# Second mixer's norm: TensorE sums each block's squares itself, with 10 waking instructions in place of 28

## Chip, cores and metric

The kernel runs on one core of a Trainium2 chip. The metric is the device time of one execution in microseconds (us). Before the change the median of three runs is 1398.13 us (1397.18 to 1398.22).

## What is computed

Two decoder layers on 512 tokens of 1024 features. Each layer is a mixer and a mixture of experts (MoE), each behind an RMS norm and with a residual; a last RMS norm follows. Layer 0's mixer is a gated MLP beside a short convolution, layer 1's is a gated linear recurrence. Cut to the part that matters here:

```python
def rms_norm(x, g):
    xf = x.astype(jnp.float32)
    y = xf * lax.rsqrt(jnp.mean(jnp.square(xf), axis=-1, keepdims=True) + EPS)
    return y.astype(x.dtype) * g

for layer in range(DEPTH):
    h = rms_norm(x, norm_mix_g[layer])
    if layer % 2 == 0:
        x = x + mixer_ab(h, ...)          # layer 0
    else:
        x = x + mixer_rglru(h, ...)       # layer 1: the "second mixer"
    h = rms_norm(x, norm_ffn_g[layer])
    x = x + hierarchical_moe(h, ...)      # 32 experts, 2 per token
return rms_norm(x, norm_final_g)
```

The change is at the RMS norm ahead of `mixer_rglru`: for every token the 1024 squares of x have to be summed.

## The kernel before

Between the stages x stands transposed, in `xT`: 8 blocks of 128 features (partitions) by 512 tokens. The stages follow each other: mixer 0 (0 to 129 us), its output projection with the routing of tokens to experts (to 198 us), MoE 0 (to 690 us), mixer 1, its projection and routing (to 896 us), MoE 1 and the last norm (to 1399 us). All weights arrive through one stream of 1 MB loads on SyncE's queue, which runs ahead through a ring of ten buffers: a load starts when the work before it has freed a slot.

**Around the change.** The last experts of MoE 0 are added to x in eight steps (`combine`, L992 and L993). Step i makes the 128x512 product `pc` of block i on TensorE (two matmuls of 512 columns, in fp32r), VectorE adds it to `xT`, and then `after(i)` runs, which here is an object of the class `Sums`. It has ScalarE square block i into `sq[i]` (four buffers, `i % 4`). The four blocks 0 to 3 are added on GpSimd into one (three additions of 128x512), the blocks 4 to 7 on VectorE into another (three more). TensorE then sums each of the two over the 128 partitions: `square_sums` (L327) makes four matmuls, one for 128 tokens each, in which the squares are the stationary 128x128 operand and the column `one` is the moving one. Every fp32 matmul of the program stands in the trace as two MATMUL and two LDWEIGHTS, so one call of `square_sums` is eight of each.

`wake(b, n)` (L170) issues n matmuls of the 128x128 identity whose result nobody reads. After the first `square_sums` stand nine (18 instructions in the trace), after the second five (10). The table `WAKE` holds these counts.

Then `rstd_of` (L308) turns the sums into 1/sqrt(mean + eps): VectorE scales the sums and adds eps (L311), ScalarE takes the root (L317), VectorE inverts it and refines it by a Newton step (L318 to L321). `Normed` spreads the result with four transposes on TensorE (`prow`, L339), `begin` adds three wakes, VectorE makes the first normed block `hh` (L348), and the first product `pu` of mixer 1 starts (L435). The same `rstd_of` serves the norm of mixer 0 (at 12 us) and the two routings (`choose`, at 186.6 and 881.1 us). Each engine runs its instructions in the order in which the program issues them.

Of the kernel before, what the change touches and what calls it, by code (L numbers as in the profile page):

```python
# [8 lines left out]
F32 = mybir.dt.float32  # L9
# [4 lines left out]
AF = mybir.ActivationFunctionType  # L14
OP = mybir.AluOpType
# [3 lines left out]
P = 128  # L19
T = 512  # L20
NT = 4
D = 1024
NJ = 8
# [6 lines left out]
EPS = 1e-6  # L30
RING = 10
AHEAD = 2
FIRST = (0, 4, 1, 5, 2, 3, 6, 7)
WAKE = (18, 7, 9, 5, 3, 16, 4)
BIG = 1.0e6
LOW = -3.0e38

# [2 lines left out]
def hybrid_trunk(ctx: ExitStack, tc: tile.TileContext, x, norm_mix_g, norm_ffn_g, norm_final_g,  # L40
# [5 lines left out]
    V, A, G, TE, SY = nc.vector, nc.scalar, nc.gpsimd, nc.tensor, nc.sync  # L46

    cons = ctx.enter_context(tc.tile_pool(name="cons", bufs=1))
# [5 lines left out]
    def bank(i, name, shape=(P, 512), dtype=F32):  # L54
        return ps.tile(list(shape), dtype, tag=f"b{i}", name=name)
# [103 lines left out]
    def buf(k, shape, name, dtype=F32):  # L159
        return big.tile([P, *shape], dtype, tag=f"q{k}", name=name)  # L160
# [5 lines left out]
    def wake(b, n):  # L166

        o = bank(b, "wake", (P, P))
        for _ in range(n):
            TE.matmul(o, ident, ident, start=True, stop=True)  # L170
# [30 lines left out]
    V.tensor_scalar(ident, ji, 0.0, None, op0=OP.is_equal)  # L201
    one = cons.tile([P, 1], F32, name="one")
    V.memset(one, 1.0)
    dummy = cons.tile([P, 1], F32, name="dummy")

    def warm(func):
# [101 lines left out]
    def rstd_of(ss, n=NT):  # L308

        ms = big.tile([P, 3, n], F32, tag="ms", name="ms", bufs=4)  # L310
        V.tensor_scalar(ms[:, 0], ss, 1.0 / D, EPS, op0=OP.mult, op1=OP.add)  # L311
        return rsqrt(ms)

    def rsqrt(ms):

        y, t = ms[:, 2], ms[:, 1]
        A.activation(t, ms[:, 0], AF.Sqrt)  # L317
        V.reciprocal(y, t)  # L318
        V.tensor_tensor(t, y, y, op=OP.mult)
        V.scalar_tensor_tensor(t, t, -0.5, ms[:, 0], op0=OP.mult, op1=OP.mult)  # L320
        V.scalar_tensor_tensor(y, t, 1.5, y, op0=OP.add, op1=OP.mult)  # L321
        return y

    def square_sums(o, sq, first, last, chunks=range(NT)):

        for c in chunks:
            TE.matmul(o[:, c:c + 1], sq[:, c * P:(c + 1) * P], one, start=first and c == 0,  # L327
                      stop=last and c == NT - 1)

    class Normed:  # L330
# [23 lines left out]
        def begin(self):  # L354
            wake(3, WAKE[4])
            self.make(0)
            self.make(1)
            for j in range(2, NJ + 1):
                later(lambda j=j: self.make(j), 2)

    def transposed_input():

        pt = bank(0, "pg0", (P, NJ))
        TE.transpose(pt, rows0, ident[0:NJ, 0:NJ])
        wake(7, WAKE[5])
        gains = cons.tile([P, NJ], F32, name="gains0")
        V.tensor_copy(gains, pt)
        ss = big.tile([P, NT], F32, tag="ss", name="ss")
        for c in range(NT):
            xc = xin[c // 2][:, c % 2, :]  # L370
            junk = big.tile([P, D], F32, tag="JK"[c % 2], name="junk")
            A.activation(junk, xc, AF.Square, accum_out=ss[:, c:c + 1])
            if c == NT - 1:
                rstd = rstd_of(ss)
            for s in range(2):
                pt = bank(1 + (2 * c + s) % 4, "pxt", (P, 4, P))
                for i in range(4):
                    TE.transpose(pt[:, i, :], xc[:, (4 * s + i) * P:(4 * s + i + 1) * P], ident)
                (A.copy if c == NT - 1 else V.tensor_copy)(xT[:, 4 * s:4 * s + 4, c * P:(c + 1) * P], pt)
        wake(7, WAKE[6])  # L380
        return Normed(rstd, gains, 5)
# [86 lines left out]
    def mixer0():  # L468
# [39 lines left out]
        def vnorm():  # L508
            V.tensor_scalar(ms[:, 0], mv[:, :, 1], 1.0, EPS, op0=OP.mult, op1=OP.add)
            r = rsqrt(ms)  # L510
            for c in range(NT):
                V.tensor_scalar(vn[c], vn[c], mv[:, c, 0:1], r[:, c:c + 1], op0=OP.subtract, op1=OP.mult)
            warm(AF.Gelu_apprx_tanh)
# [197 lines left out]
    class Moe:  # L711
# [23 lines left out]
        def sm(self, *shape):  # L735

            n = 1
            for d in shape:
                n *= d
            k = 0 if self.used[0] + n <= 512 else 1  # L740
            t = self.rt[k][:, self.used[k]:self.used[k] + n]
            self.used[k] += n
            assert self.used[k] <= 512
            if len(shape) == 1:
                return t
            names = "abcd"[:len(shape)]
            return t.rearrange(f"p ({' '.join(names)}) -> p {' '.join(names)}",
                               **{k: d for k, d in zip(names, shape)})
# [42 lines left out]
        def choose(self):  # L791

            sm = self.sm
            lg, gm = sm(NT, 36), sm(NT)
            self.rstd = rstd_of(self.ss)
            for c in range(NT):
                V.scalar_tensor_tensor(lg[:, c], self.pl[:, c], self.rstd[:, c:c + 1], self.brow, op0=OP.mult, op1=OP.add)
# [20 lines left out]
            V.tensor_tensor(self.eb, self.e12[:, 0], self.e12[:, 1], op=OP.add)  # L818
            wake((self.b0 + 7) % 8, WAKE[0])

# [51 lines left out]
        def gates(self):  # L872

            sm, pr = self.sm, self.pr
            for cc in range(NT):
                TE.matmul(pr[:, NT, :], ones, self.eb[:, cc, :], start=(cc == 0), stop=(cc == NT - 1))
            wake((self.b0 + 7) % 8, WAKE[1])
            cnt, nb, ends, adj, one32 = sm(NE), sm(NE), sm(NE), sm(NE), sm(NE)
# [321 lines left out]
    class Sums:  # L1200


        def __init__(self, b):
            self.o = bank(b, "pss", (P, NT))
            self.sq = {}

        def __call__(self, i):
            self.sq[i] = buf(i % 4, (T,), "sq")
            A.activation(self.sq[i], xT[:, i, :], AF.Square)
            for e, a, b in {1: [(G, 1, 0)], 3: [(G, 3, 2), (G, 3, 1)], 7: [(V, 5, 4), (V, 7, 6), (V, 7, 5)]}.get(i, []):  # L1210
                e.tensor_tensor(self.sq[a], self.sq[a], self.sq[b], op=OP.add)
            if i == 7:
                square_sums(self.o, self.sq[3], True, False)
                wake(1, WAKE[2])
                square_sums(self.o, self.sq[7], False, True)
                wake(1, WAKE[3])

    y = mixer0()
    late = []
# [7 lines left out]
    if stop in ("m0", "e0"):  # L1227
        return store()
    y = mixer1(rstd_of(late[0].o))

    if stop == "m1":
# [103 lines left out]
```

## Time and profile before

| what | value |
|---|---|
| median of three runs | 1398.13 us |
| profiled execution, its own time | 1400.72 us |
| its span, first to last instruction | 1399.0 us |
| TensorE (PE) busy | 1329.5 us, 95% of the span |
| VectorE (DVE) busy | 592.9 us, 42% |
| ScalarE (ACT) busy | 350.4 us, 25% |
| GpSimd (POOL) busy | 88.9 us, 6% |
| bytes moved | 436.95 MB, 312 GB/s on the mean |

The durations in the rows below come from the one profiled execution. It is 2.59 us longer than the median, so a sum made from its rows is a difference against 1400.72 us and is carried over to the median. PEld is TensorE's loading of stationary operands, which overlaps PE. [...] In a timeline row the time in brackets is how long the engine stood idle before it, and behind the arrow is what ended the wait.

### The profile page before, as it was taken

What the parts mean: (1) busy time and instruction counts of PE and PEld (TensorE: products, weight loads), DVE (VectorE), ACT (ScalarE), POOL (GpSimd) and SP (SyncE); (2) the same over time, 40 slices, a digit from 0 to 9 for tenths busy, and PEclk for the clock granted to TensorE, in tenths of its full rate; (3) what the DMA queues carried; (4) which work ended last, traced back from release to release, by engine and by line L of the source; (5) the groups of instructions that cost most, each with busy time, mean ns of one, the idle gap of its engine ahead of it and who ended that gap; (6) DMA issues with size and microseconds to landing.
All of it is one profiled execution on the core that took longest, in us unless ns stands there. A gap on an engine that the chain in (4) does not pass through costs nothing. (4 is left out here: it accounts for less than half of the span.)

```text
span 1399.0 us, 16628 instructions
## 1 busy us (share of the span) xinstructions
PE 1329.5 (95%) x6674; PEld 765.5 (55%) x6674; DVE 592.9 (42%) x1112; ACT 350.4 (25%) x592; POOL 88.9 (6%) x68
## 2 busy tenths in 40 slices
PE   9999999999999999998899889899999999999985
PEld 7888874554445544442587568645544455444432
DVE  5455462334423332322458784723333233323226
ACT  4335431221111111110247653212111111111113
POOL 0000100000000000000114332300000000000002
PEclk9999999999999999999799989999999999999997
DMA  9631169899999999999850025698999999999993
GB/s 356 184 110 60 61 227 339 348 409 409 409 408 409 409 409 409 409 409 409 299 180 0 0 75 209 219 342 345 409 409 409 409 408 409 409 409 409 409 409 142
DMA packets 126691, 436.95 MB, mean 312 GB/s; under 512 B 11284, under 2 KB 13968, under 8 KB 126608
## 3 DMA queue, kind: packets, MB, share of 16 engines
q1 hardware_dynamic: 126608, 435.82, 80.1%
q8 instruction: 55, 0.90, 0.3%
q14 instruction: 28, 0.23, 0.0%
HBM read 433.69 MB, written 2.10 MB: 311 GB/s over the span
## 5 line engine op out<-in xcount | busy, mean ns | idle before, releaser
L1008 PE MATMUL pu<-w,xt 128*64 128x512 f32 x1024 | 234.3, 597 | 20.8 <-DMA w<-in_moe_w_up_dram 20.7
L1008 PE MATMUL pg<-w,xt 128*64 128x512 f32 x1024 | 228.8, 597 | 1.2 <-DMA w<-in_moe_w_gate_dram 1.2
L1008 PE MATMUL pd<-w,hT 128*64 128x512 f32 x1024 | 226.8, 595 | 1.4 <-ACT hT L1032 1.4
L1026 DVE SCALAR_TENSOR_TENSOR hid<-pu,gs,sg 128x512 f32<-128x512 f32 x32 | 24.0, 751 | 365.6 <-PE pu L1008 245.1
L1008 PEld LDWEIGHTS pu<-w,xt 128*64 128x64 f32 x1024 | 70.0, 137 | 178.9 <-issue 120.6
L1008 PEld LDWEIGHTS pg<-w,xt 128*64 128x64 f32 x1024 | 72.8, 137 | 144.9 <-issue 134.5
L1008 PEld LDWEIGHTS pd<-w,hT 128*64 128x64 f32 x1024 | 70.7, 137 | 140.3 <-issue 129.4
L870 ACT ACTIVATE xt<-px,gcol 128x256 f32<-128x256 f32 x128 | 60.9, 476 | 303.4 <-PE px L868 303.3
L867 PE MATMUL px<-st,xh 128*128 128x256 f32 x512 | 132.8, 294 | 2.4 <-DVE st L857 2.0
L868 PE MATMUL px<-st,xl 128*128 128x256 f32 x512 | 126.6, 283 | 0.0
L867 PEld LDWEIGHTS px<-st,xh 128*128 128x128 f32 x512 | 97.9, 191 | 30.4 <-issue 26.2
L1048 ACT ACTIVATE y<-pd,gs 128x512 fp32r<-128x512 f32 x64 | 43.8, 687 | 264.6 <-PE pd L1008 263.2
L1049 DVE SCALAR_TENSOR_TENSOR y<-pd,gs,y 128x512 fp32r<-128x512 f32 x64 | 47.9, 750 | 140.9 <-ACT y L1048 138.4
L993 DVE TENSOR_TENSOR xT<-pc,xT 128x512 f32<-128x512 f32 x128 | 81.4, 684 | 57.0 <-PE pc L992 57.0
L993 DVE TENSOR_TENSOR rows<-pc,rows 128x512 f32<-128x512 f32 x128 | 81.4, 684 | 53.0 <-PE pc L992 53.0
L868 PEld LDWEIGHTS px<-st,xl 128*128 128x128 f32 x512 | 97.9, 191 | 1.6
L391 ACT CAST wh<-w 128x512 fp32r<-128x512 f32 x104 | 64.1, 619 | 68.3 <-PE pu L435 41.3
L392 DVE TENSOR_TENSOR wl<-w,wh 128x512 fp32r<-128x512 f32 x79 | 55.2, 701 | 50.8 <-PE pu L435 26.8
L435 PE MATMUL pu<-hh,wh 128*128 128x512 f32 x256 | 73.6, 409 | 2.5 <-ACT wh L391 2.0
L691 PE MATMUL po<-y,wh 128*128 128x512 f32 (+1 forms) x288 | 70.0, 385 | 5.0 <-ACT y L464 4.1
L992 PE MATMUL pc<-sp,y 128*128 128x512 f32 x256 | 69.6, 405 | 4.9 <-issue 4.9
L992 PE MATMUL pc<-y,sp 128*128 128x512 f32 x256 | 69.1, 403 | 2.2 <-DVEq L1137 2.2
(255 smaller groups left out, 1369.3 us busy)
## 6 DMA issues: line engine op xcount, KB each, us to landing
w<-in_moe_w_gate_dram SPq DMA_DIRECT2D x128, 1024.0 KB, 18.4
w<-in_moe_w_up_dram SPq DMA_DIRECT2D x128, 1024.0 KB, 18.3
w<-in_moe_w_down_dram SPq DMA_DIRECT2D x128, 1024.0 KB, 18.4
w<-in_ab_w_in_dram SPq DMA_DIRECT2D x10, 1024.0 KB, 15.1
w<-in_c_w_in_dram SPq DMA_DIRECT2D x8, 1024.0 KB, 10.9
w<-in_ab_w_out_dram SPq DMA_DIRECT2D x4, 1024.0 KB, 10.3
w<-in_c_w_out_dram SPq DMA_DIRECT2D x4, 1024.0 KB
xin<-in_x_dram SPq DMA_DIRECT2D x4, 512.0 KB, 6.7
```

What stands on the lines that cost most here:

```text
L391: A.copy(wh, w)
L392: lo.tensor_tensor(wl, w, f(wh), op=OP.subtract)
L435: TE.matmul(o[m], a[:, m * P:(m + 1) * P], b[:, j, :], start=first and i == 0, stop=last and i == 2)
L691: TE.matmul(o[m, i], w[:, kk, :], part(js[4 * kh + kk])[:, h], start=kh + k + kk == 0, stop=(kh, k, kk) == (1, 2, 3))
L867: TE.matmul(px, self.xh[:, c, j, :], st(c), start=(c == 0), stop=False)
L868: TE.matmul(px, self.xl[:, c, j, :], st(c), start=False, stop=(c == NT - 1))
L870: A.activation(self.xt[q][:, j, :], px, AF.Copy, scale=g)
L992: TE.matmul(pc, a, b, start=(n == 0), stop=(n == 1))
L993: V.tensor_tensor(d, pc, d, op=OP.add)
L1008: TE.matmul(o[64 * s:64 * s + 64, :], xt[:, 64 * s:64 * s + 64], w[s][:, j, wide], start=first, stop=last)
L1048: A.activation(yh[s], pd[s], AF.Copy, scale=by(0))
L1049: V.scalar_tensor_tensor(yl[s], pd[s], by(0), f(yh[s]), op0=OP.mult, op1=OP.subtract)
```

## The change

`Sums` no longer adds squares on GpSimd and VectorE. TensorE sums each of the eight blocks by itself, into the same four columns of PSUM: at step i (from 3 on) it sums block i-3, and after the last step the blocks 5, 6 and 7. That is 32 matmuls where there were 8 (64 MATMUL and 64 LDWEIGHTS in the trace, not 16). One `wake` of five matmuls stands behind them, where there were nine and five. In `rstd_of` ScalarE takes the root from the sums directly (`scale=1/D`, `bias=eps`), beside VectorE's scaling and no longer after it; this holds for all four norms that call it.

```diff
-WAKE = (18, 7, 9, 5, 3, 16, 4)
+WAKE = (18, 7, 5, 5, 3, 16, 4)
...
+    eps = cons.tile([P, 1], F32, name="eps")
+    V.memset(eps, EPS)
...
     def rstd_of(ss, n=NT):
         ms = big.tile([P, 3, n], F32, tag="ms", name="ms", bufs=4)
+        A.activation(ms[:, 1], ss, AF.Sqrt, scale=1.0 / D, bias=eps)
         V.tensor_scalar(ms[:, 0], ss, 1.0 / D, EPS, op0=OP.mult, op1=OP.add)
-        return rsqrt(ms)
+        return newton(ms)
 
     def rsqrt(ms):
+        A.activation(ms[:, 1], ms[:, 0], AF.Sqrt)
+        return newton(ms)
+
+    def newton(ms):
         y, t = ms[:, 2], ms[:, 1]
-        A.activation(t, ms[:, 0], AF.Sqrt)
...
+        def add(self, i):
+            square_sums(self.o, self.sq[i], i == 0, i == NJ - 1)
+
         def __call__(self, i):
             self.sq[i] = buf(i % 4, (T,), "sq")
             A.activation(self.sq[i], xT[:, i, :], AF.Square)
-            for e, a, b in {1: [(G, 1, 0)], 3: [(G, 3, 2), (G, 3, 1)], 7: [(V, 5, 4), (V, 7, 6), (V, 7, 5)]}.get(i, []):
-                e.tensor_tensor(self.sq[a], self.sq[a], self.sq[b], op=OP.add)
-            if i == 7:
-                square_sums(self.o, self.sq[3], True, False)
-                wake(1, WAKE[2])
-                square_sums(self.o, self.sq[7], False, True)
-                wake(1, WAKE[3])
+            if i > 2:
+                self.add(i - 3)
+            if i == NJ - 1:
+                for k in range(NJ - 3, NJ):
+                    self.add(k)
+                wake(3, WAKE[2])
```

TensorE's order at the end of MoE 0, from the fourth product `pc` to the first product of mixer 1. In these rows a matmul is counted as written, so an fp32 one is a single x1 here and two instructions in the trace. Before:

```order
L992 MATMUL pc_4853<-sp,y 128x512 x2
L992 MATMUL pc_4861<-sp,y 128x512 x2
L992 MATMUL pc_4867<-sp,y 128x512 x2
L992 MATMUL pc_4873<-sp,y 128x512 x2
L992 MATMUL pc_4879<-sp,y 128x512 x2
L327 MATMUL pss<-one,sq 128x1 x4
L170 MATMUL wake<-ident 128x128 x9
L327 MATMUL pss<-one,sq 128x1 x4
L170 MATMUL wake<-ident 128x128 x5
L339 MATMUL prow<-ident,ms 128x128 x4
L170 MATMUL wake<-ident 128x128 x3
L435 MATMUL pu_4926<-hh,wh 128x512
```

The same stretch of TensorE now:

```order
L999 MATMUL pc_4854<-sp,y 128x512 x2
L334 MATMUL pss<-one,sq 128x1 x4
L999 MATMUL pc_4864<-sp,y 128x512 x2
L334 MATMUL pss<-one,sq 128x1 x4
L999 MATMUL pc_4874<-sp,y 128x512 x2
L334 MATMUL pss<-one,sq 128x1 x4
L999 MATMUL pc_4884<-sp,y 128x512 x2
L334 MATMUL pss<-one,sq 128x1 x4
L999 MATMUL pc_4894<-sp,y 128x512 x2
L334 MATMUL pss<-one,sq 128x1 x16
L170 MATMUL wake<-ident 128x128 x5
L346 MATMUL prow<-ident,ms 128x128 x4
```

Four of the sums now stand between the last five products, and four behind them; the nine wakes are gone.

VectorE's order at the same place, from its seventh addition to x to the end of the norm. Before:

```order
L993 TENSOR_TENSOR xT<-pc_4873,xT 128x512
L993 TENSOR_TENSOR xT<-pc_4879,xT 128x512
L1211 TENSOR_TENSOR sq<-sq 128x512 x3
L311 TENSOR_SCALAR ms<-pss 128x4
L318 RECIPROCAL ms<-ms 128x4
L319 TENSOR_TENSOR ms<-ms 128x4
```

The same stretch of VectorE now:

```order
L1000 TENSOR_TENSOR xT<-pc_4884,xT 128x512
L1000 TENSOR_TENSOR xT<-pc_4894,xT 128x512
L314 TENSOR_SCALAR ms<-pss 128x4
L325 RECIPROCAL ms<-ms 128x4
L326 TENSOR_TENSOR ms<-ms 128x4
```

The three additions are gone from VectorE (and three from GpSimd's queue). The order of the other instructions is the same on every engine.

## Rows read from the trace of the kernel before

**Rows 1.** Windows by stage: us, busy us (count) per engine, PEclk, DMA share, GB/s.

```profile
760.00:810.00 50.00, 43.44 (x164) 30.74 (x164) 42.19 (x49) 30.92 (x48) 19.90 (x14) 0.97 0.00 0
...
930.00:980.00 50.00, 50.00 (x272) 25.54 (x269) 14.65 (x26) 9.52 (x18) 0.00 (x0) 1.00 0.91 352
980.00:1100.00 120.00, 120.00 (x620) 60.00 (x619) 42.28 (x75) 19.59 (x35) 0.00 (x0) 1.00 1.03 409
```

**Rows 2.** Waits of SyncE's queue: waiter, waited for, us in total, times, longest.

```profile
SPq L120 <- DVE y L465: 110.1, 1, 110.1
```

**Rows 3.** Timeline, end of MoE 0 to mixer 1: start, us, engine, line, operation, tiles.

```profile
683.33 6.28 PE L992 MATMUL pc<-sp,y 128*128 128x512 f32 x16 [4.87 <-issue]
...
684.59 0.69 DVE L993 TENSOR_TENSOR xT<-pc,xT 128x512 f32<-128x512 f32 x1 [4.40 <-PE pc L992]
...
685.44 0.69 DVE L993 TENSOR_TENSOR xT<-pc,xT 128x512 f32<-128x512 f32 x1 [0.16 <-PE pc L992]
...
691.26 1.31 PEld L327 LDWEIGHTS pss<-one,sq 128*128 128x128 f32 x8 [2.09 <-POOL sq L1211]
...
692.46 3.96 PEld L170 LDWEIGHTS wake<-ident 128*128 128x128 f32 x18
...
693.37 1.42 DVE L1211 TENSOR_TENSOR sq<-sq 128x512 f32<-128x512 f32 x2 [0.77 <-ACT sq L1209]
...
696.30 1.83 PEld L327 LDWEIGHTS pss<-one,sq 128*128 128x128 f32 x8
...
698.00 2.25 PEld L170 LDWEIGHTS wake<-ident 128*128 128x128 f32 x10
...
698.25 0.16 DVE L311 TENSOR_SCALAR ms<-pss 128x4 f32<-128x4 f32 x1 [3.47 <-PE pss L327]
...
698.68 0.18 DVE L318 RECIPROCAL ms<-ms 128x4 f32<-128x4 f32 x1 [0.27 <-ACT ms L317]
...
699.29 0.16 DVE L321 SCALAR_TENSOR_TENSOR ms<-ms 128x4 f32<-128x4 f32 x1
...
700.13 0.87 PEld L339 LDWEIGHTS prow<-ident,ms 128*128 128x128 f32 x4
...
702.31 0.76 PEld L435 LDWEIGHTS pu<-hh,wh 128*128 128x128 f32 x4
```

**Rows 4.** Windows around that stretch, columns as in rows 1.

```profile
681.60:688.30 6.70, 4.97 (x12) 3.91 (x13) 3.07 (x5) 2.76 (x6) 1.29 (x1) 0.50 0.56 155
688.40:691.80 3.40, 1.74 (x10) 1.18 (x9) 2.18 (x4) 1.29 (x4) 2.55 (x2) 1.00 1.06 377
691.90:702.00 10.10, 10.10 (x48) 10.10 (x49) 4.06 (x10) 1.84 (x4) 0.00 (x0) 0.50 1.05 387
702.10:710.00 7.90, 7.90 (x37) 6.40 (x37) 6.08 (x11) 3.43 (x6) 0.00 (x0) 1.00 1.04 386
```

**Rows 5.** The third window, instructions of line L327 alone: us, PE, PEld, PEclk.

```profile
691.90:702.00 10.10, 2.47 (x12) 2.50 (x12) 0.50 1.05 387
```

**Rows 6.** Timeline at the routing of layer 0, where PEclk is 1.00.

```profile
185.03 0.58 PE L327 MATMUL misc<-one,sq 128*128 128x1 f32 x4
...
185.48 0.61 PE L758 MATMUL misc<-wr,xT 128*128 128x36 f32 x4
...
186.55 0.16 DVE L311 TENSOR_SCALAR ms<-misc 128x4 f32<-128x4 f32 x1 [1.25 <-PE misc L327]
186.75 0.20 ACT L317 ACTIVATE ms<-ms 128x4 f32<-128x4 f32 x1 [1.00 <-DVE ms L311]
...
186.98 0.18 DVE L318 RECIPROCAL ms<-ms 128x4 f32<-128x4 f32 x1 [0.27 <-ACT ms L317]
```

**Rows 7.** Timeline at the norm of mixer 0.

```profile
11.95 0.16 DVE L311 TENSOR_SCALAR ms<-ss 128x4 f32<-128x4 f32 x1
...
12.38 0.18 DVE L318 RECIPROCAL ms<-ms 128x4 f32<-128x4 f32 x1 [0.27 <-ACT ms L317]
...
12.59 0.16 DVE L319 TENSOR_TENSOR ms<-ms 128x4 f32<-128x4 f32 x1
```

## Prediction

> **What bounds the kernel now.** I read the windows by stage first, then SyncE's waits, then the timeline where the change sits, and last the granted clock there.
>
> The windows ask whether time lost or won near 690 us reaches the end. From 980 us on the weight stream runs at 409 GB/s, its flat rate, but between 760 and 810 us it moves nothing, and between 930 and 980 us it makes 352 GB/s with TensorE busy in all 50.00 us [rows 1]. In between the stream waits for buffers, once for 110.1 us, until a late piece of mixer 1 has been written [rows 2]. So the loads of MoE 1 are released by mixer 1 and by the first experts, and whatever delays mixer 1 delays them by as much. The reader should see that the saturated stream later on is no cushion: it starts later too.
>
> The timeline shows the way to mixer 1 [rows 3]. The eight products start at 683.33, 0.85 us apart (the additions at 684.59 and 685.44). The first sum over partitions waits for GpSimd, to 691.26. The second has its squares at 694.79 (693.37 + 1.42), but TensorE is still in the 18 waking instructions until 696.30. Its last load ends where the next wake's begins, at 698.00. Behind it stand ten waking instructions to 700.13, the transposes, three more wakes, and the first product of mixer 1 loads at 702.31. From 691.26 on this is TensorE's own queue, instruction behind instruction.
>
> The clock decides what each costs [rows 4]. TensorE ran at half clock (0.50) to 688.3, at full clock for 3.4 us, and again at 0.50 from 691.9 to 702.0, although it was busy in all 10.10 of those 10.10 us. What it did then was sums (2.47 us, [rows 5]), wakes and transposes. The clock had come back at 688.4 after five microseconds of 512-column products alone; it came back at 702.1 after four of wakes and transposes alone. The one spell with sums among the wakes did not bring it back.
>
> **The change part by part.**
>
> *The price of a sum.* One block is eight instruction pairs. At half clock the second group's loads begin at 696.30 and the next load behind them at 698.00: 1.70 us for eight, 0.2125 us each [rows 3]. At full clock four pairs take 0.45 us (185.03 to 185.48), 0.1125 us each [rows 6]. The time goes into the 128x128 load, since only one column streams. So 64 pairs cost 13.6 us at half clock and 7.2 us at full; the 16 of before were 3.4 and 1.8.
>
> *Which clock.* I take half clock for the whole stretch. It starts at half clock, as before, since nothing ahead of 683.33 changes there. Before, the clock rose after the products had run back to back from the first to nearly the last. Now the fourth product is followed by a sum, and from there on 1.70 us of sum stand to 0.85 us of product. Sums in a full queue left the clock at 0.50 for 10 us [rows 4, 5].
>
> [...]
>
> *The sum at half clock.* Four products from 683.33 end near 686.9 (4 x 0.85, and 0.15 for the first one's start). Then four pairs of sum and product, 4 x (1.70 + 0.85) = 10.2, to 697.1. Then four sums in a row, 32 x 0.2125 = 6.8, to 703.9. Before, this point was 698.00. TensorE's queue is **5.9 us** later. Its inputs are not late: block 7 is added to x about 1 us after the last product and squared by 699, while TensorE reaches its sum only at 702.2.
>
> Two things the trace of before does not show. The first load of a sum may slip under the product ahead of it, up to 0.21 us in each of five places: down to 4.9. The product's first load now stands behind a sum with nothing to hide it, up to 0.21 in each of four: up to 6.7. They pull against each other, and I take 5.9.
>
> [...]
>
> *The removed additions.* Three on GpSimd and three on VectorE were what the first sum waited for until 691.26, and part of what the second waited for. They go from the path, but TensorE is late next: its work from 683.33 is now longer than the whole chain was. Worth nothing, and no one else waits for these engines there.
>
> *The wakes.* Eighteen instructions go (their 3.8 us lay between the sums; their end is in the 698.00 that I compare with). Ten stay, still ahead of the transposes: 2.13 us. So the stretch from the end of the sums to the first product stays 4.31 us (698.00 to 702.31). In it the clock was back at 702.04 or so, just in time. Now it may come back up to 1.1 us later (five microseconds of dense work, not four, [rows 4]), and products in that time run at half speed: 0 to 0.6 us more.
>
> *The root on ScalarE.* VectorE's chain was 698.25 to 698.68 for scaling and root, where 0.43 becomes about 0.23. But its result was ready at 699.45 and the transposes waited for the wakes until 700.13 [rows 3]. The wakes cover the gain: nothing here. At the two routings the same step goes from 0.43 (186.55 to 186.98) to about 0.23, and there ScalarE stood idle for 1.00 us ahead of it [rows 6] and VectorE goes on from the inverse to the choice of experts: 0.2 us each. At mixer 0's norm VectorE comes late to the scaling, so the root is long done and the inverse follows at VectorE's own pitch of 0.2 us, not at 0.43 [rows 7]: 0.23 us. Together **-0.6 us**, and 0 if something else is late there. The constant `eps` costs one small fill in the first microseconds, beside the loads of x.
>
> *Sum.* 5.9 - 0.6 = **+5.3 us**. Against the profiled execution's own 1400.72 that is 1406.0; carried to the median 1398.13 it is **1403.4**. With the ends of the terms, 4.9 - 0.6 = 4.3 to 6.7 + 0.6 = 7.3, the forecast's own range is 1402.4 to 1405.4. The profile is 2.59 us above the median. If part of that is the clock having stood higher here in the timed runs, the loss is larger, so I widen the upper end to 1406.5.
>
> **The rivals.**
>
> *Full clock (faster).* The clock returns at 688.4 as before and stays. By then 1.5 of the first sum's 1.7 us are done. The rest is 0.1 + 4 x 0.43 + 7 x 0.90 = 8.1, to 696.5: 1.5 us earlier than 698.00. The wakes shrink from 2.13 to 1.1, the four transposes by 0.4: together -2.9, with the root -3.5, or **1394.6**. For it: TensorE never idles here, while before its loads stood idle for 2.09 us ahead of 691.26 [rows 3]. Against it: the rows of 10 busy us at 0.50. It decides once the sums count for the clock as products do. Chance 0.08.
>
> *One spell.* The four products alone, or with a bit of the first sum, lift the clock once, and it falls again as it did at 691.9. A spell of 3.4 us [rows 4] does the work of 6.8: +5.3 - 3.4 = +1.9, **1400.0**. For it: products alone did lift it, after 5 us; against: they now run alone for only 3.6. Chance 0.12. The same time would come out if two loads slipped under each of the eight 512-column matmuls that now stand among sums (16 x 0.2125 = 3.4); nothing in the rows shows a load that far ahead. Chance 0.04.
>
> *Absorbed.* The delay is taken up by the stream in MoE 1, **1397.5** with the root's gain. Rows 1 and 2 speak against it, since the stream waits for mixer 1. Chance 0.04.
>
> **How the numbers follow.** The forecast has 0.72, full clock 0.08, one spell and hidden loads 0.16, absorbed 0.04. Differences under 0.2% (2.8 us) can hardly be told from none. Faster: 0.08. Within 0.2%: 0.16 + 0.04 = 0.20. Slower: 0.72. The range for 8 in 10 takes the forecast's and reaches down over about half of the one-spell case: 1399.8 to 1406.5.
>
> **What would show it.** In the changed kernel's profile: PEclk 0.50 from 682 to about 706 in the windows; a sum of eight loads 1.7 us long each time; TensorE idle nowhere between 684 and 706; the five wakes beginning near 704, not at 698; the first product of mixer 1 near 708; from there on the same distances as before, with the stream in MoE 1 starting some 6 us later; the inverse 0.2 us behind the scaling at the norms. I am wrong if the clock stands at 1.00 among the sums, or if the eight loads of a sum take well under 1.7 us at 0.50.

## The result and the profile after

The changed kernel takes 1405.33 us (median of four runs, 1405.12 to 1406.91), the kernel before 1397.8 us in the same comparison: **1.0054 of it, with a 95% interval of 1.0041 to 1.0066**. That is 7.5 us slower. The profiled execution of after took 1405.2 us, its span is 1403.4 us.

Windows of after around the change, columns as in rows 1 (compare rows 4). PEclk is the clock granted to TensorE, as a share of its full clock:

```profile
683.60:686.80 3.20, 3.20 (x11) 2.53 (x9) 2.40 (x4) 1.71 (x3) 0.00 (x0) 0.50 0.76 208
687.00:690.20 3.20, 3.20 (x26) 3.03 (x26) 1.55 (x3) 1.26 (x2) 0.00 (x0) 1.00 1.11 345
690.40:703.90 13.50, 13.50 (x61) 13.14 (x60) 3.11 (x9) 2.53 (x5) 0.00 (x0) 0.50 1.05 387
704.10:710.00 5.90, 5.90 (x29) 4.70 (x28) 4.68 (x9) 2.29 (x4) 0.00 (x0) 1.00 1.02 375
```

TensorE is busy in every microsecond from 683.6 to 710.0. Its clock rises once, to 1.00 at 686.9, and falls at 690.3, in the middle of sums and products that follow each other without a gap. In all 13.50 us of the third window it is 0.50.

The timeline of after there, columns as in rows 3:

```profile
683.03 3.41 PE L999 MATMUL pc<-sp,y 128*128 128x512 f32 x8 [4.72 <-issue]
...
686.24 1.27 PE L334 MATMUL pss<-one,sq 128*128 128x1 f32 x8
...
689.06 1.09 PEld L334 LDWEIGHTS pss<-one,sq 128*128 128x128 f32 x8
...
690.47 2.04 PEld L334 LDWEIGHTS pss<-one,sq 128*128 128x128 f32 x8
...
690.89 1.70 PE L334 MATMUL pss<-one,sq 128*128 128x1 f32 x8
...
693.45 6.82 PE L334 MATMUL pss<-one,sq 128*128 128x1 f32 x32
...
700.07 2.25 PEld L170 LDWEIGHTS wake<-ident 128*128 128x128 f32 x10
...
700.31 0.26 ACT L313 ACTIVATE ms<-pss,eps 128x4 f32<-128x4 f32 x1 [5.20 <-PE pss L334]
...
700.61 0.16 DVE L314 TENSOR_SCALAR ms<-pss 128x4 f32<-128x4 f32 x1 [6.22 <-ACT ms L313]
...
702.20 0.87 PEld L346 LDWEIGHTS prow<-ident,ms 128*128 128x128 f32 x4
...
704.37 0.76 PEld L442 LDWEIGHTS pu<-hh,wh 128*128 128x128 f32 x4
```

Eight loads of a sum span 1.09 us between two products at full clock and 2.04 at half (the first of them overlaps the product ahead; the eight matmuls of that sum take 1.70). The 32 pairs behind the last product take 6.82 us (0.213 each). The wakes begin at 700.07, 2.07 us later than before [rows 3], and the first product of mixer 1 at 704.37, 2.06 us later.

The rest of the loss stands some 680 us later, at the end of MoE 1, where the change edits nothing. First TensorE's row of the first additions there, before, then after:

```profile
1379.87 5.70 PE L992 MATMUL pc<-y,sp 128*128 128x512 f32 x16 [2.23 <-DVEq L1137]
```

```profile
1383.82 4.80 PE L999 MATMUL pc<-y,sp 128*128 128x512 f32 x14 [4.84 <-issue]
```

TensorE idles 2.23 us ahead of them in the one, waiting for VectorE's queue, and 4.84 us in the other, for nothing that the profile shows as a releaser. What stands in that gap is the end of a loop that is skipped here (`tc.For_i`, for experts with too many tokens). Its branches on TensorE's queue, by line, before and after: count, then duration in ns as least/median/most, first and last start in us.

```profile
L1137 PEldq COMPARE_BRANCH  x3: 70/181/395, 1374.0 to 1379.6; - x3
```

```profile
L1144 PEldq COMPARE_BRANCH  x3: 82/187/3413, 1375.4 to 1383.6; - x3
```

One branch takes 3413 ns where before none took over 395. The row of the DMA queue that carries instructions (packets, MB, share), before and after:

```profile
q8 instruction: 55, 0.90, 0.3%
```

```profile
q8 instruction: 56, 0.92, 0.3%
```

One more packet of some 16 KB (0.92 MB / 56): the change makes 60 more rows on TensorE and its queue (13561 for 13501), and the code behind them moves along by as much. (e6 below has 56 packets too, and not this wait.) That the slow branch waits for code to arrive is the author's reading; the profile names no releaser. The trace agrees with it here: the slow branch runs from 1379.18 to 1382.59, and a packet of 16384 bytes on queue q8 moves from 1380.11 to 1381.24 (one of 8192 on q14, the other instruction queue, in the same stretch). Windows of after across the branch, columns as in rows 1, show data moving in that stretch of it alone:

```profile
1379.20:1380.10 0.90, 0.00 (x0) 0.00 (x0) 0.79 (x2) 0.52 (x1) 0.00 (x0) 1.00 0.00 0
1380.10:1381.25 1.15, 0.00 (x0) 0.00 (x0) 0.62 (x4) 0.17 (x1) 0.00 (x0) 1.00 0.08 21
1381.30:1382.60 1.30, 0.00 (x0) 0.00 (x0) 0.00 (x0) 1.26 (x2) 0.00 (x0) 1.00 0.00 0
```

Whether the place of the code decides this is what e5, e6 and e9 below test.

Split at the same four points, in us from the trace ("additions" is the first product `pc` at MoE 0's end, "mixer 1" its first product `pu`). Before was profiled a second time, as e4 below.

| stretch | before | before again (e4) | after | sums alone (e1) |
|---|---|---|---|---|
| start to additions | 683.33 | 683.18 | 683.03 | 683.03 |
| additions to mixer 1 | 19.01 | 16.40 | 21.37 | 24.77 |
| mixer 1 to last expert product of MoE 1 | 674.71 | 674.14 | 673.99 | 672.93 |
| that product to the additions behind it | 2.82 | 2.82 | 5.43 | 5.25 |
| to the end | 19.16 | 19.15 | 19.60 | 19.62 |
| span | 1399.03 | 1395.69 | 1403.42 | 1405.60 |

Against before's second profile after loses 7.73 us, close to the 7.53 us between the medians: 4.97 in the stretch that the change edits, 2.61 in the wait at MoE 1's end, 0.45 behind it, and -0.30 in the rest.

### The profile page after: what moved, and what is told of

Same layout as the page of the kernel before. It is cut to its first block, busy times and chain, and to the rows that moved or that the text cites. A ratio compares the mean times of both kernels' runs of the same rounds, so it can differ in the third digit from the quotient of the medians.

```text
span 1403.4 us, 16684 instructions
## 1 busy us (share of the span) xinstructions
PE 1332.9 (95%) x6704; PEld 768.9 (55%) x6704; DVE 591.0 (42%) x1110; ACT 351.2 (25%) x592; POOL 84.6 (6%) x65
## 6 DMA issues: line engine op xcount, KB each, us to landing
w<-in_ab_w_out_dram SPq DMA_DIRECT2D x4, 1024.0 KB, 10.1
```

## The experiments

Theory (as predicted): the 64 pairs of load and one-column matmul run at half clock, and mixer 1 starts later by as much. Rivals: the root does it or hides something, the place of the code does it, or the base is at fault.

### Each part alone, and the kernel before once more

**e1**, the sums as after, the root as before:

```diff
-        A.activation(ms[:, 1], ss, AF.Sqrt, scale=1.0 / D, bias=eps)
-        return newton(ms)
+        return rsqrt(ms)
```

> The change's sums and its single wake, with the root taken after VectorE's scaling as before. Theory (the sums on TensorE at half clock carry the whole loss, the root on ScalarE gives back 0.4 to 0.6 us): 1405.3 + 0.5 = about 1405.8 us, 1.0057 of before. Rival (the new root is slower at the routings, since VectorE's scaling there now waits for ScalarE, and carries part of the loss): about 1404.5 us or less.

Measured: 1407.23 us, 1.0070 of before (1.0052 to 1.0087). One window of its trace, and two of VectorE's additions in its timeline:

```profile
682.10:709.20 27.10, 26.17 (x103) 24.37 (x104) 9.25 (x18) 5.95 (x11) 0.00 (x0) 0.50 0.97 340
```

```profile
689.41 0.69 DVE L999 TENSOR_TENSOR xT<-pc,xT 128x512 f32<-128x512 f32 x1 [1.87 <-PE pc L998]
...
691.97 0.69 DVE L999 TENSOR_TENSOR xT<-pc,xT 128x512 f32<-128x512 f32 x1 [1.87 <-PE pc L998]
```

This execution is the forecast as it was written: 0.50 over all of the 27 us, and a step of 2.56 us (691.97 - 689.41; forecast 1.70 + 0.85). The stretch is 24.77 us, 5.76 longer than the 19.01 of before. So the sums carry the loss, without the root. The wait at MoE 1's end is in this run too (5.25 us against 2.82 in the table above), with as many rows on TensorE and its queue as in after (13561).

**e2**, the other part alone: before with ScalarE's root; its sums and wakes stay.

```diff
...
+        A.activation(ms[:, 1], ss, AF.Sqrt, scale=1.0 / D, bias=eps)
         V.tensor_scalar(ms[:, 0], ss, 1.0 / D, EPS, op0=OP.mult, op1=OP.add)
-        return rsqrt(ms)
+        return newton(ms)
...
```

> The change's root on ScalarE alone; squares, additions and wakes as before. Theory: 0.4 us off mixer 0's norm, 0.05 off each routing, nothing at mixer 1 where the wakes cover it: 0.5 us less than before, about 1397.3. Rival (it does not show): 1397.8.

Measured: 1396.54 us, 0.9991 (0.9982 to 1.0001). The interval holds the forecast gain (0.6 us would be 0.9996) and also none, so this run does not tell the two apart.

**e4**, the kernel before without an edit, run as if it were another.

> The kernel before, unchanged, timed and profiled once more. Its first profile took 1400.72 us, 2.9 us more than the median of its timed runs, 1397.8. Theory (the granted clock between 688 and 702 us is not the same in every execution, and the first profile shows a costly case): a profile nearer 1397.8 us in which TensorE has the full clock for part of 691.9 to 702.0 and mixer 1 starts 2 to 4 us earlier. Rival (the weight stream of the MoE stages ran a little slower in that one execution): 0.50 in that stretch again, and the difference lies between 200 and 680 or after 900 us.

Measured: 1397.69 us, 0.9995 (0.9986 to 1.0005). Its windows, as rows 4:

```profile
682.20:688.90 6.70, 5.72 (x14) 4.52 (x15) 3.65 (x6) 2.79 (x5) 1.76 (x2) 0.50 0.73 208
689.10:692.30 3.20, 1.88 (x13) 1.39 (x13) 2.10 (x4) 1.37 (x4) 1.88 (x2) 1.00 1.05 388
692.50:695.70 3.20, 3.20 (x16) 3.20 (x16) 1.38 (x2) 0.34 (x1) 0.00 (x0) 0.50 1.05 387
695.90:702.00 6.10, 5.77 (x40) 4.90 (x39) 4.14 (x11) 1.86 (x4) 0.00 (x0) 1.00 1.05 387
```

The same instructions as in rows 4, but the second spell at 0.50 lasts 3.4 us, not 10.1, and the stretch takes 16.40 us, not 19.01. The profile that the prediction rests on had drawn a costly case: 1400.72 us is above all of the 25 timed runs of before in this comparison (1396.47 to 1400.23). The stretches of e2 (16.33), e5 (16.34) and e11 (16.89), which have before's sums, lie at e4's; that of e9, which has them too, takes 15.29. So the stretch with before's sums varies by up to 3.7 us between profiles (in e5 and e9 it stands behind a shorter wait at MoE 0's end), and 19.01 is the longest of them.

### Why the clock falls

**e3**: the sums of after, with the same loads in the same order, but each matmul streams 128 columns of ones, not one.

```diff
...
+    def wide_sums(o, sq, first, last):
+
+        for c in range(NT):
+            TE.matmul(o[:, c * P:(c + 1) * P], sq[:, c * P:(c + 1) * P], one.to_broadcast([P, P]),
+                      start=first and c == 0, stop=last and c == NT - 1)
...
-            self.o = bank(b, "pss", (P, NT))
+            self.o = bank(b, "pss", (P, T))
...
-            square_sums(self.o, self.sq[i], i == 0, i == NJ - 1)
+            wide_sums(self.o, self.sq[i], i == 0, i == NJ - 1)
...
-    y = mixer1(rstd_of(late[0].o))
+    y = mixer1(rstd_of(late[0].o.rearrange("p (c k) -> p c k", k=P)[:, :, 0]))
...
```

> The changed kernel, but each sum streams the column of ones 128 times (a 128x128 result, of which one column is read), as a wake does; loads, order and number of instructions stay. Theory (it is the single streamed column that lets the clock fall, not the loads): a pair costs the same 0.21 us at half and 0.11 at full clock, the clock returns between 686 and 691 and stays at 1.00 to mixer 1, the sums end near 696 in place of 700, the first product of mixer 1 starts 5 to 8 us earlier than in the changed kernel: 1397 to 1400 us. Rival (the clock falls whatever the sums stream, as soon as the 512-column products thin out): 0.50 to about 704 as in the changed kernel, 1405 us or a little more.

Measured: 1400.40 us, 1.0019 (1.0009 to 1.0028). Windows and the last sums in its trace:

```profile
683.80:687.00 3.20, 3.20 (x10) 2.57 (x9) 2.44 (x4) 1.76 (x3) 0.00 (x0) 0.50 0.76 211
687.20:699.00 11.80, 11.43 (x91) 10.71 (x90) 5.40 (x13) 3.93 (x7) 0.00 (x0) 1.00 1.07 376
```

```profile
692.18 3.73 PE L340 MATMUL pss<-one,sq 128*128 128x128 f32 x32
```

The clock rises at 687.1 as in after, and does not fall again before 772. The 32 pairs take 3.73 us, not 6.82, and the stretch 15.50 us, not 21.37. Loads, order and count are after's; what differs is the columns streamed, and with them the width of the result. At full clock the wider matmul costs next to nothing: a step of product and sum takes 1.36 us here (688.30 to 689.66 by VectorE's additions) and 1.35 in after's full-clock spell (688.13 to 689.48). So TensorE's being busy, or without gaps, was not what kept the clock: after was busy in 13.50 of 13.50 us at 0.50.

What is left of e3's loss is the wait at MoE 1's end: its longest branch there takes 3493 ns. Without it an estimate is 1400.4 - 2.6 = 1397.8, which would be before's time.

**e7** sums pairs: GpSimd adds blocks 0 and 1, 2 and 3, VectorE 4 and 5, 6 and 7; four sums of one column each, so half of after's loads. **e8** is e7 with 128 columns per matmul.

```diff
-            if i > 2:
-                self.add(i - 3)
+            if i in (1, 3):
+                G.tensor_tensor(self.sq[i], self.sq[i], self.sq[i - 1], op=OP.add)
+            if i in (4, 6):
+                square_sums(self.o, self.sq[i - 3], i == 4, False)
...
+                for k in (5, 7):
+                    V.tensor_tensor(self.sq[k], self.sq[k], self.sq[k - 1], op=OP.add)
+                    square_sums(self.o, self.sq[k], False, k == 7)
```

> The changed kernel, but neighbouring blocks are added in pairs first (two additions on GpSimd, two on VectorE), so that TensorE sums four blocks with 32 pairs of instructions, two behind products 4 and 6 and two at the end; five wakes; four instructions fewer on TensorE than the kernel before. Theory (what costs is the sums' length at half clock): from the first product of the additions to the first of mixer 1 16 to 18.5 us, between before's two profiles, no wait for code at the end: 1396 to 1398.5 us. Rival (interleaved sums lose the clock for good): 19 to 20 us, 1400 or more.

> The same with sums that stream the column 128 times, as in e3_wide. Theory: the clock stays at 1.00 through most of the stretch, 14.5 to 15.5 us from the first product of the additions to the first of mixer 1, no wait for code at the end: about 1395 us. Rival (the gaps in which TensorE waits for GpSimd and VectorE let the clock fall all the same): 17 us or more, 1397 to 1399 us.

Measured: e7 1400.58 us, 1.0019 (1.0009 to 1.0028), a miss of what was expected; e8 1394.58 us, 0.9981 (0.9972 to 0.9991). One window each, first e7, then e8:

```profile
689.60:703.00 13.40, 12.02 (x50) 10.93 (x50) 6.57 (x14) 2.66 (x5) 0.00 (x0) 0.50 1.05 387
```

```profile
685.00:698.00 13.00, 10.28 (x69) 8.59 (x68) 8.77 (x18) 5.21 (x10) 2.55 (x2) 1.00 1.07 372
```

In e7 halving the loads did not keep the clock: it fell again, at 689.5 (after: 690.3), and the stretch took 18.98 us. In e8 TensorE is less busy (10.28 of 13.00 us, e7's 12.02 of 13.40) and stays at 1.00; its stretch takes 14.58 us. That is e3's finding a second time, 4.4 us apart for the columns alone. In all, the three profiles with 128 columns (e3, e8, and e10 below) hold 1.00 to mixer 1 once it is there, and the four with one column and sums between the products (after, e1, e7, and e6 below) stand at 0.50 for 13 us or more.

**e11**: before with two wakes between its sums, not nine, to see whether the wakes that the change drops were worth anything.

```diff
-WAKE = (18, 7, 9, 5, 3, 16, 4)
+WAKE = (18, 7, 2, 5, 3, 16, 4)
```

> The kernel before with two wakes between its two sums, not nine (14 instructions fewer in the trace, 28 with their loads). Theory (at half clock the nine hold up the second sum from 694.8 to 696.3, at full clock not at all): 0 to 1.5 us less than before, 1396.5 to 1398. Rival (they keep the clock, and without them it is at 0.50 until mixer 1 more often): 1398.5 to 1400. The branch stands at 239 at the end of MoE 1 and should take 0.4 us.

Measured: 1398.23 us, 1.0003 (0.9994 to 1.0013), no difference. TensorE now idles 1.81 us ahead of the second sum, waiting for VectorE's additions, and the clock stood at 0.50 from 693.8 to 700.6; the stretch is 16.89 us, e4's 16.40. Dropping these wakes was neither the loss nor a gain.

### The wait at MoE 1's end

**e5**: before, with 15 more wakes inside MoE 0, whose results nobody reads either, to move the code behind them. **e9** is e5 with one wake more (8 and 8). **e6** does the same to after, with 49 (9 and four times 10).

```diff
+                    if n == 3 and self.l == 0 and p in {13: 8, 14: 7}:
+                        wake(4, {13: 8, 14: 7}[p])
```

> The kernel before with 15 more wakes (60 instructions on TensorE, as many as the change adds net) among the last experts of MoE 0, at places where TensorE waits for weights anyway. Theory (the 2.5 us that the changed kernel loses between the last expert of MoE 1 and the eight additions is TensorE's branch over the skipped loop waiting for code, and 60 instructions earlier in the program shift that code): the branch takes 3.3 to 3.5 us in place of 0.4, 5.3 to 5.5 us from the last expert's product to the first addition's in place of 2.82, and 1400.4 to 1400.8 us. Rival (that delay comes from the sums, by the clock or by the weight stream): 0.4 us, 2.82 us, 1398.0.

> The kernel before with 16 wakes among the last experts of MoE 0, one more than e5_before_padded. In the built programs the place of TensorE's branch over the skipped loop, counted in instructions modulo 256, is at the end of MoE 0 179 (before, changed), 113 (e6) and 236 (e5), and at the end of MoE 1 11 (before), 71 (changed), 5 (e6), 68 (e5); the branch took 3.3 to 3.7 us at 71, 113 and 179 and 0.3 to 0.4 us at 5, 7, 11, 68 and 236. Here it is 240 and 72. Theory (code comes in blocks of 256 instructions, and the branch waits when its target lies beyond the next block): 0.4 us at MoE 0's end and 3.4 us at MoE 1's, where e5 took 0.3: 2.6 us more than e5, about 1398.5. Rival (the wait has another cause that the extra wakes only moved): 0.3 to 0.4 us at both, 1396.

> The changed kernel with 49 more wakes among the experts of MoE 0 (196 instructions, with the change's 60 together 256). Theory (code position, and code comes in pieces of that many instructions): the branch at the end of MoE 1 is back at 0.4 us, 2.82 us from the last expert to the first addition, about 1402.5 to 1403 us. Rival: 3.4 us, 5.4 us and 1405.3 us, or more by the wakes.

Measured: e5 1395.91 us, 0.9985 (0.9975 to 0.9995); e9 1397.10, 0.9995 (0.9985 to 1.0004); e6 1404.03, 1.0043 (1.0029 to 1.0058). The branches on TensorE's queue, in e6 at MoE 1's end, in e5 at MoE 0's end, in e9 at MoE 1's end:

```profile
L1146 PEldq COMPARE_BRANCH  x3: 70/181/407, 1375.4 to 1381.0; - x3
```

```profile
L1139 PEldq COMPARE_BRANCH  x3: 104/187/407, 676.1 to 681.6; - x3
```

```profile
L1139 PEldq COMPARE_BRANCH  x3: 70/304/2093, 1367.5 to 1373.1; - x3
```

e6 is the clear case: after's work with the code moved on, and the 3413 ns are 407, the gap 2.83 us and not 5.43. In its trace the wait is gone; in the times e6's ratio is 0.0011 lower than after's, with intervals that overlap. e5 did not bring the wait to MoE 1's end, as was expected of it: its 15 wakes made 57 more instructions, not 60 (a few waits went), and its branch there is quick, 309 ns. But it took away a wait that before has too, at the end of MoE 0: 407 ns for 3441, and the additions begin 2.83 us after the last expert's product, not 5.46. Of these 2.6 us the times show 1.6 (1395.91 for 1397.48); in its trace the last expert's product comes 1.15 us later than before (679.02 for 677.87), which takes part of the gain back. e9, one wake on, has the wait at MoE 1's end as was expected, but on the last of the three branches, where after has it on the second, and with 2.09 us, not 3.4; its gap is 4.74 us, and its time is 1397.10 us where 1398.5 was expected.

The packets on q8 agree with a wait for code, too. The thirteen traces hold 14 slow branches at the ends of the two MoEs (2.09 to 3.78 us), and in each of the 14 such a packet lands 1.35 to 1.38 us before the branch ends. In e9 it started 0.26 us before the branch, in the other 13 waits 0.92 to 1.46 us after its begin. (The last packet on q14 lands 0.4 to 1.9 us before the end, in no fixed step.) Where the longest branch is quick, the last packet on q8 had landed at least 1.8 us before it began.

The place of the first of these branches among TensorE's instructions in the built programs, modulo 256, orders all that was seen. That code comes in blocks of 256 instructions, as the theories of e6 and e9 have it, was not shown. The nearest figure of the traces is lower: 13501 rows on TensorE and its queue over 55 packets of 16384 bytes on q8 are 245 a packet in before, 13561 over 56 are 242 in after.

| place | kernel and stage | longest branch |
|---|---|---|
| 5, 7, 11 | e6; e7 and e8; before (e2 and e4 too), all at MoE 1 | 407; 395 and 313; 395 ns |
| 64, 68 | e10, e5, at MoE 1 | 309, 309 ns |
| 71, 72 | after, e1 and e3; e9, all at MoE 1 | 3413, 3313 and 3493; 2093 ns |
| 113, 179 | e6; before (e4 too), after, e1, e2, e3, e7, e8, e11, at MoE 0 | 3729; 3281 to 3781 ns |
| 236, 239, 240 | e5 and e10 at MoE 0; e11 at MoE 1; e9 at MoE 0 | 407; 395; 312 ns |

At the places from 71 to 179 that were seen the branch waits, at the others it does not. Where exactly the line runs, what sets it, and why e9 pays at the last branch, stays open. The distance to the end of the loop does not give it: that end lies 389 instructions on in the built programs, in the next block of 256 from 71 and two blocks on from 236.

### A version that beats both

**e10**: e8 with e5's 15 wakes, so pairs, 128 columns, and the branches of both stages at quick places.

> e8_pairs_wide with 15 wakes among the last experts of MoE 0, so that the two branches stand at 236 and 64. Theory (both effects are independent): both branches at 0.4 us, the stretch from the first product of the additions to the first of mixer 1 at 14.5 us as in e8, together 2.6 us less than e8: about 1392 us, 0.996 of before. Rival (the earlier start of the additions is eaten by the clock, which then falls later): 1394 to 1395.

Measured: **1392.87 us** (1390.14 to 1393.46), 0.9956 of before (0.9942 to 0.9971). Its window over the whole stretch:

```profile
678.00:698.00 20.00, 14.42 (x87) 11.80 (x86) 13.49 (x28) 9.08 (x16) 2.50 (x2) 1.00 0.75 253
```

No half clock in it; the stretch takes 13.88 us (680.32 to 694.20), and the additions begin 2.83 us after the last expert product at MoE 0 (5.46 before) and 2.82 after it at MoE 1.

## Why the prediction was right, and where not

1403.4 us was forecast and 1405.33 measured, inside the range. Several steps were off, and they partly cancel: the spell at full clock took 3.4 us from the forecast, the base and a wait at a skipped loop that stood in no term added 2.6 us each (1403.4 - 3.4 + 2.6 + 2.6 = 1405.2). That the total fell into the range is in part luck; the mechanism, sums that run at half clock and push mixer 1 back, is what the runs show.

- **Price of a sum: right.** 0.2125 us a load at half clock and 0.1125 at full were taken from rows 3 and 6. After has 6.82 / 32 = 0.213 at half, and e1's step is 2.56 us. The two unseen terms (a load under the product ahead, a product's own load) cancel within 0.01 us, as was taken.
- **Half clock: right in its sign and cause, not throughout.** "Half clock for the whole stretch" is e1's execution. In after's own profile the "one spell" rival came true: 1.00 from 686.9 to 690.3, worth 24.77 - 21.37 = 3.4 us, just the size worked out for it. With it came the prediction's own sign of being wrong, 1.00 among the sums. The step that failed is that the products run alone for too short a time: the clock was back 3.9 us after the first of them, not 5.1 as before. The rival's time, 1400.0, did not follow, because of the next two points.
- **Base: the term that was mis-sized.** The 5.9 us were counted from a profile in which before itself stood at 0.50 for 10 us. Against e4 the forecast's own case costs 24.77 - 16.40 = 8.4 us where 5.9 was forecast, and the one-spell case 21.37 - 16.40 = 5.0. The prediction subtracted 2.59 us to reach the median and then added the full difference. It named this ("the loss is larger") and widened the upper end for it, but kept the middle. The two profiles of before differ by 2.6 us in this stretch, as much as the 2.59 us.
- **End of MoE 1: a missing term.** "From there on the same distances as before" failed at one place: the wait at the slow branch, 5.43 - 2.82 = 2.6 us. Nothing in the sum or the rivals stood for it. It was in reach: before's own trace has a branch of 3441 ns at MoE 0's end. The first profile's 2.06 us at mixer 1 and this 2.61 make 4.7 us; the small terms take 0.3 back, and the two spans differ by 4.4.
- **Delay passed on: right.** Mixer 1's first product to MoE 1's first is 193.72 us before and 193.63 after. In e1 it is 192.64, so there 1.1 us came back, and e1's MoE 1 takes 480.29 us (480.98 before). The "absorbed" rival had no more than these 1.8 us of 5.8.
- **Wakes: right.** From the wakes' begin to `pu` it is 4.31 us before and 4.30 after (700.07 to 704.37). The clock was back at 704.0, in time. In e1 it came back at 709.3, 5.8 us after the wakes' begin at 703.47, where before it took 4.0: 1.8 us later and not 1.1 at most, so there products ran at half clock.
- **Root: the right total, wrong places.** At the routing, rows of after as in rows 6:

```profile
187.04 0.26 ACT L313 ACTIVATE ms<-misc,eps 128x4 f32<-128x4 f32 x1 [0.80 <-PE misc L334]
...
187.34 0.16 DVE L314 TENSOR_SCALAR ms<-misc 128x4 f32<-128x4 f32 x1 [1.55 <-ACT ms L313]
187.42 0.17 DVE L325 RECIPROCAL ms<-ms 128x4 f32<-128x4 f32 x1
```

VectorE's scaling was forecast to run beside the root. It waits for it: 1.55 us idle, ended by ScalarE's `ms`. So 0.38 us (187.04 to 187.42) stand where 0.43 stood, and 0.05 is won at each routing, not 0.2. Both write into one tile and read the same sums; which of the two makes the wait was not tried. At mixer 0's norm VectorE comes late, as said, and there the gain is larger than the 0.23 forecast. After's rows, as in rows 7:

```profile
12.85 0.16 DVE L314 TENSOR_SCALAR ms<-ss 128x4 f32<-128x4 f32 x1
12.91 0.17 DVE L325 RECIPROCAL ms<-ms 128x4 f32<-128x4 f32 x1
...
13.73 0.54 PE L346 MATMUL prow<-ident,ms 128*128 128x128 f32 x3 [0.39 <-DVE ms L328]
```

Before, the transposes stood here:

```profile
13.21 0.65 PE L339 MATMUL prow<-ident,ms 128*128 128x128 f32 x4 [0.76 <-DVE ms L321]
```

The inverse begins 0.06 us behind the scaling, not 0.2. From the scaling to the transposes it is 0.88 us, where before it was 1.26 (11.95 to 13.21). Together 0.38 + 0.1 = 0.5, for 0.6 forecast, which no time here can tell from none (e2). At mixer 1 the wakes cover it, as said; the same wait stands in after's row at 700.61.

- **Additions removed: right.** TensorE is late next, and idles nowhere from 683.6 on.
- **Full clock rival.** It was to come "once the sums count for the clock as products do". e3 has that clock with 128 columns streamed, and its stretch, 15.50 us, is 3.5 us under 19.01, near the rival's 2.9 (its 3.5 holds the root's 0.6, which is won elsewhere). Counted from e4's 16.40 the same stretch wins 0.9 us only, and the wait at the slow branch takes more than that (2.6 us).

Busy time alone did not decide the clock, as the prediction read from rows 4: 13.50 busy us of 13.50 at 0.50 in after, 10.28 of 13.00 at 1.00 in e8.

## What to carry to other kernels

A sum over partitions with one moving column cost as much here as one with 128 columns at full clock (steps of 1.35 and 1.36 us), so its price was that of its load (eight loads span 1.09 us in both). Among sums of one column TensorE's clock fell to 0.50, whether the engine was busy in 13.50 of 13.50 us (after) or in 12.02 of 13.40 (e7); with 128 columns it stayed at 1.00 (11.43 of 11.80 us in e3, 10.28 of 13.00 in e8). So look at PEclk and at the shape of the matmuls, not at the busy share alone. Before a base profile carries a sum, look whether its costly spell is there in a second profile of the same kernel. And a change that adds or drops instructions moves all code behind it: at a skipped loop far from the edit TensorE won or lost up to 2.6 us by that in the traces. Unused instructions alone did it: e5 and e6 lose a slow branch (407 ns in place of 3441 and of 3413), e9 gains one (2093 in place of 395).

## What was not expected of the hardware

- The longest branch at a skipped loop took 0.3 to 0.4 us or 2.1 to 3.8 us on TensorE's queue, by the place of the code: e5 and e9 differ by one wake, and have 309 and 2093 ns at MoE 1's end.
- Each of the 14 slow branches ended 1.35 to 1.38 us after a packet of 16384 bytes on instruction queue q8 had landed.
- Before's clock in this stretch differed between two executions of the same program (0.50 for 10.1 us or for 3.4 us), worth 2.6 us of 1398.
- Eight pairs with 128 columns cost nearly the same at full clock as with one (steps of 1.36 and 1.35 us).
